# Attention with a step's scores ahead of the preceding pair's transposes and weighted sums, and the right side's tiles at multiples of 256 bytes

## The chip, the cores and the metric

The kernel runs on one core of a Trainium2 chip. The metric is the device time of one execution in microseconds (us). The core has five engines that work at the same time, each through its own list of instructions in order: TensorE (PE) multiplies matrices and also transposes, with PEld as the row of its weight loads; VectorE (DVE) and ScalarE (ACT) do element-wise work and are the only ones that the kernel lets read PE's results; GpSimd (POOL) does element-wise work on SBUF; SyncE (SP) issues most DMAs. SBUF is the on-chip memory of 128 partitions; PSUM holds PE's results in eight banks.

## The reference, cut to what matters

With DEPTH 1 the trunk is a single layer: RMSNorm, 2-D neighbourhood attention and a residual, then RMSNorm, SwiGLU and a residual, then a final RMSNorm. It is applied to a prompt of 1024 tokens and a sample of 512, both of width 1024, on a grid of 64 columns.

```
def neighbourhood_attention(x, w_qkv, rpb, w_o):
    ...
    def row_step(r):
        rs = jnp.clip(r - kh // 2, 0, rows - kh)
        ...
        s = jnp.einsum('bjqhd,bkjchd->bhjqkc', qr, kr).astype(jnp.float32) * scale
        ...
        s = jnp.where(valid_j, s + bias.astype(jnp.float32), -jnp.inf)
        p = jax.nn.softmax(s.reshape(B, NA_HEADS, NA_NCB, NA_QBW, kh * NA_KBW), axis=-1)
        p = p.reshape(s.shape).astype(x.dtype)
        return jnp.einsum('bhjqkc,bkjchd->bjqhd', p, vr)
    o = lax.map(row_step, jnp.arange(rows))
    o = jnp.moveaxis(o, 0, 1).reshape(B, T, D_MODEL)
    return o @ w_o

def swiglu(x, w_gate, w_up, w_down):
    return (jax.nn.silu(x @ w_gate) * (x @ w_up)) @ w_down
```

Sixteen heads of 64 attend within 8 rows; columns are handled in four blocks of 16 queries, each with a band of 32 keys. The values are 32-bit floats.

## The kernel before, in words

**Precision.** Every large product is made of three matmuls on rounded operands: each operand is split into a high part (a cast on ACT) and a low part (the difference, on DVE; `split`, L139 to L145), and `PASS` (L164) names the three pairs of parts.

**Stages.** By the span of the profile: norms, transposes and value projections up to 181 us (`v_tile`, matmuls L281; the values go to HBM as `v_d`); prompt attention from 181 to 519; sample attention from 519 to about 732, with the output projection (`project`, L593) woven in and going on to 797; gate and up products to 1466 (`product`, L824, seven products of a Strassen-like scheme); down products to the end (L1062).

**A step of attention.** `steps` yields, for one head pair `hp` and one group `g` of 8 query rows, two steps. A step holds two units (two column blocks `j`), and each unit two heads. A unit's work is:

- `scores` (L391): for each head three matmuls into a PSUM bank of tag S (L397); then, per head, one reduction on DVE that adds the bias, writes the tile `s` to SBUF and takes the row's extreme (L405), an exponential on ACT with its sum (L408), a reciprocal (L410), and a scaling, on DVE for the first head (L412) and on ACT for the second (L414);
- `flip` (L418): per head three transposes (two for the sample) into an S bank (L423), then the two halves of the eviction to the tile `pT`: the cast on ACT (L426) and the difference on DVE (L427);
- `weighted` (L431): matmuls with the values into two banks of tag V (L434), which both units of the step share.

`collect` (L438) then sums the parts of a step's two V banks: a copy on ACT to `tmp` (L444) and two additions on DVE (L445, L447) to the output tile `oT`, which POOL's queue stores to HBM as `o_d` (L462) when the second step of a group is done.

There are four S banks. A step's scores take all four, and the transposes take all four again. There are two tiles of each kind of output and temporary, and four tiles `s`.

**The order of a step.** `step` (L477) traces: the scores and the softmax of this step's two units; filler; the weighted sums and the collect of the *preceding* step, whose transposes are already in `pT`; then, unit by unit, this step's transposes, each followed by filler. Filler is PE work that does not depend on the step: portions of 6 matmuls of the next head pair's q and k projections (`proj`, L335), and in the sample of the output projection (L593). For a prompt head pair `fill` runs two portions after the scores and one after each unit's transposes.

**What sets the order on the engines.** The program is traced in the order of the Python code. A list scheduler then orders each engine's instructions by their place in the trace and by its own estimate of when inputs and buffers will be ready, so an instruction that it takes to be waiting can be overtaken by later ones of the same engine. On the chip each engine runs its list in order; semaphores guard each use of a buffer.

**Between the steps** `chores` load and split weights and values: `v_split` waits for the DMA of a value tile `vr` from `v_d` (L381; cast at L141 on ACT, difference at L142 on DVE), and `wsplit` splits a weight block into `whl`.

**SBUF.** Pools stand on two sides: most grow up from the bottom, those with `side="right"` down from the top. The first tile of the right side is `edge`, 24 floats for each partition (L89), which nothing reads. Below it lie, in their time, `hTp` (the prompt's normed and transposed tokens), `wo` and `oh`, then `hx`, a part of the weight tiles of the gate and up products (`a2p`, `r2p`, `t4p`), and in the last stage `go`, `gr` and the first three of `wd` and `dr` (`rt`). On the left are among others `hTs`, `whl`, all tiles of attention, `h`, and the rest of `wa`, `ws`, `wd`.

Of the kernel before, what the change touches and what calls it, by code (L numbers as in the profile page):

```python
# [11 lines left out]
F32 = mybir.dt.float32  # L12
# [6 lines left out]
P = 128  # L19
# [36 lines left out]
def body(tc, xp, xs, g_mix, g_ffn, g_fin, w_qkv, rpb, w_o, w_g, w_u, w_d, yp, ys):  # L56
# [8 lines left out]
    es = ExitStack()  # L65
    with es:
# [21 lines left out]
        ident = cpool.tile([P, P + 16], F32, name="ident")[:, :P]  # L88
        edge = es.enter_context(tc.tile_pool(name="edge", bufs=1, side="right")).tile([P, 24], F32, name="edge")  # L89
        nc.gpsimd.memset(edge, 0.0)  # L90
# [300 lines left out]
        def scores(q, k, krow, nrow, j, bias):  # L391
            n = nrow * 32
# [9 lines left out]
            for h, pt in enumerate(pss):  # L402
                s = ap.tile([P, 384], F32, tag="s", name="s", bufs=4)
                mx = stat.tile([P, 1], F32, tag="mx", name="mx")
# [32 lines left out]

        def collect(pos, dst):  # L438
            for h in range(2):
                m, o = (0, HD) if h == 0 else (HD, 0)  # L440
                pv = pos[h].rearrange("p (g z q) -> p g z q", g=2, z=2)
                tmp = ap.tile([P, 2, P], F32, tag="tmp", name="tmp")
                t = tmp[m:m + HD]
                nc.scalar.copy(t, pv[o:o + HD, :, 0])  # L444
                nc.vector.tensor_tensor(t, t, pv[m:m + HD, :, 0], ALU.add)  # L445
                tv = t.rearrange("p g (r i) -> p g r i", i=16)
                nc.vector.tensor_tensor(dst(h), tv, pv[m:m + HD, :, 1].rearrange("p g (r i) -> p g r i", i=16),  # L447
                                        ALU.add)

        def steps(hp, g, q, k, v, n, store):  # L450

            oT = ap.tile([P, 512], F32, tag="o", name="oT", bufs=2)
            ov = oT.rearrange("p (r j i) -> p j r i", r=8, j=NJ)
# [23 lines left out]
        def step(st, fill):  # L477
# [6 lines left out]
            if prev:  # L484
                p, pT = prev.pop()
                pos = [psum("V", "po") for _ in range(2)]
# [3 lines left out]
                if p["done"]:  # L490
                    p["done"]()
            pT = []
            for u, x in enumerate(ss):
                pT.append(flip(x, st["n"]))
                fill(1 + u)
            if st:
                prev.append((st, pT))

# [40 lines left out]
        for hp in range(HP):  # L539
# [13 lines left out]
            def fill(part):  # L553
                run(fillers, 1 if part or last else 2)

# [57 lines left out]
        for hp in range(HP):  # L613
# [7 lines left out]
            def fill(part):  # L621
                run(fillers, 1 if part else 2)
                run(ofill, 1 if part else 2)

# [501 lines left out]
```

## Time and profile before

| | |
|---|---|
| time, median of 3 runs | 1808.15 us (1807.66 to 1812.14) |
| the profiled execution | 1815.71 us |
| its span, first to last instruction | 1813.8 us |
| PE busy | 1749.2 us, 96% |
| DVE busy | 1215.9 us, 67% |
| ACT busy | 870.6 us, 48% |
| POOL busy | 431.2 us, 24% |
| mean granted PE clock | 0.992 |

The span is what the trace shows; the execution's own time has a little around it. The share of busy time is a mean over stages of very different make-up. PE's matmuls are pipelined: one is shown as lasting longer than the distance to the next one's start, so busy time alone does not tell how fast they follow each other. In rows of the timeline the first number is the start, the second the length, `x` the count of merged instructions, and a bracket at the end gives the idle time ahead of the row and what ended it. In rows of waits, the engine and the tile that waited stand left of the arrow, what ended the wait on the right.

### The profile page before, as it was taken

Reading aid. Unit: us, or ns where it says so; the run is one execution under the profiler, and the core shown is the slowest. Engines: PE = TensorE matmul, PEld = TensorE weight load, DVE = VectorE, ACT = ScalarE, POOL = GpSimd, SP = SyncE. Lnnn points to the kernel's source line nnn. Section 1 sums busy time; section 2 is a strip of 40 time slices with the busy share of each in tenths; the row PEclk is TensorE's granted clock in tenths of the full one; section 3 lists DMA queues with packets and bytes.
Section 4 is the critical chain, followed back from the end, with each engine's and each line's share of the span. In section 5 each row is a group of like instructions: output and inputs, shape, how many; then the busy total and the mean of one; then the engine's idle time right before and its main releaser. Section 6 shows DMA issues by size and latency. Waiting matters only on the chain.

```text
span 1813.8 us, 25894 instructions
## 1 busy us (share of the span) xinstructions
PE 1749.2 (96%) x9178; PEld 1527.3 (84%) x9178; DVE 1215.9 (67%) x2267; ACT 870.6 (48%) x1742; POOL 431.2 (24%) x509
## 2 busy tenths in 40 slices
PE   7999999999999999999999999989999999999998
PEld 6888777777777788779999999888999987888886
DVE  4401878788787666667877777988777756446553
ACT  4411777667785555544444445433344335433423
POOL 1111000000130000112424242565424352005300
PEclk9999999999999999999999999999999999999999
DMA  7755333333464453653553634888433269555633
GB/s 237 224 182 168 98 107 109 108 103 106 131 204 149 135 157 111 193 181 119 177 171 111 216 109 146 284 298 275 137 115 122 75 210 324 180 158 165 206 110 107
DMA packets 229858, 295.60 MB, mean 163 GB/s; under 512 B 27648, under 2 KB 173824, under 8 KB 229728
## 3 DMA queue, kind: packets, MB, share of 16 engines
q1 hardware_dynamic: 205744, 215.94, 39.3%
q0 software_dynamic: 21248, 69.62, 10.5%
q10 hardware_dynamic: 2736, 8.39, 1.5%
q8 instruction: 72, 1.18, 0.3%
q14 instruction: 58, 0.48, 0.1%
HBM read 218.45 MB, written 87.97 MB: 169 GB/s over the span
## 4 chain that ended last, share of the span: by engine, by line
PE 69%; DMA 11%; DVE 9%; ACT 4%; issue 4%; SPq 2%; POOL 2%; DVEq 0%; ACTq 0%; POOLq 0%
PE pa L824 16%; PE pd L1062 16%; PE pd L824 8%; PE pg L335 7%; PE pgv L281 7%; DMA vr<-v_d 5%; PE pgo L593 4%; PE pb L824 4%; PE pss L397 3%; SPq L381 2%; PE po L434 1%; PE ptt L423 1%; DMA gr<-gop_d 1%; DMA wt_d<-t 1%; ACT s L408 1%
## 5 line engine op out<-in xcount | busy, mean ns | idle before, releaser
L1062 PE MATMUL pd<-wd,go 128*128 128x512 f32 x1386 | 325.7, 396 | 3.6 <-DVE wd L142 2.6
L1062 PEld LDWEIGHTS pd<-wd,go 128*128 128x128 f32 x1386 | 260.4, 188 | 68.8 <-DVE wd L142 4.9
L824 PE MATMUL pa<-h,ws 128*128 128x384 f32 x1056 | 199.4, 336 | 8.7 <-ACT c L849 7.2
L335 PE MATMUL pg<-hTp,whl 128*128 128x512 f32 x768 | 201.9, 407 | 0.0
L824 PE MATMUL pd<-h,ws 128*128 128x384 f32 x1056 | 197.6, 334 | 0.0
L824 PEld LDWEIGHTS pa<-h,ws 128*128 128x128 f32 x1056 | 183.1, 188 | 12.0 <-ACT c L849 9.2
L824 PEld LDWEIGHTS pd<-h,ws 128*128 128x128 f32 x1056 | 184.3, 188 | 0.0
L142 DVE TENSOR_TENSOR ws<-wt,ws 128x1024 fp32r<-128x1024 f32 x88 | 109.9, 1250 | 90.9 <-ACT ws L141 90.9
L335 PEld LDWEIGHTS pg<-hTp,whl 128*128 128x128 f32 x768 | 139.2, 190 | 34.2 <-issue 7.7
L824 PE MATMUL pa<-h,wa 128*128 128x384 f32 x792 | 151.1, 343 | 8.3 <-DVE c L856 8.3
L824 PEld LDWEIGHTS pa<-h,wa 128*128 128x128 f32 x792 | 141.4, 191 | 10.5 <-DVE c L856 10.5
L593 PE MATMUL pgo<-wo,oh 128*128 128x512 f32 x576 | 139.0, 392 | 1.4 <-DVE oh L142 1.4
L141 ACT CAST go<-gr 128x768 fp32r<-128x768 f32 x84 | 65.7, 782 | 151.6 <-PE pd L1062 106.7
L408 ACT ACTIVATE s<-s,mx 128x384 f32<-128x384 f32 (+1 forms) x192 | 109.1, 570 | 54.8 <-DVE mx L405 54.8
L142 DVE TENSOR_TENSOR wa<-wr,wa 128x512 fp32r<-128x512 f32 x132 | 124.0, 952 | 13.1 <-ACT wa L141 12.1
L142 DVE TENSOR_TENSOR go<-gr,go 128x768 fp32r<-128x768 f32 x84 | 81.6, 972 | 75.0 <-ACT go L141 73.4
L593 PEld LDWEIGHTS pgo<-wo,oh 128*128 128x128 f32 x576 | 107.4, 188 | 24.4 <-DVE oh L142 1.8
L889 POOL DMA_DIRECT2D gop_d<-c x66 | 50.6, 766 | 313.1 <-DVE c L880 313.1
L141 ACT CAST wa<-wr 128x512 fp32r<-128x512 f32 x132 | 81.8, 621 | 88.5 <-PE pb L824 43.5
L141 ACT CAST ws<-wt 128x1024 fp32r<-128x1024 f32 x88 | 92.4, 1051 | 63.3 <-issue 49.7
L335 PE MATMUL pg<-hTs,whl 128*128 128x512 f32 x384 | 105.7, 411 | 2.0 <-DVE q L346 2.0
L824 PE MATMUL pb<-h,wa 128*128 128x384 f32 x528 | 101.0, 339 | 4.3 <-ACT wa L141 4.1
(158 smaller groups left out, 2945.3 us busy)
## 6 DMA issues: line engine op xcount, KB each, us to landing
wr<-ffn_w_gate SPq DMA_DIRECT2D x44, 512.0 KB
wr<-ffn_w_up SPq DMA_DIRECT2D x44, 512.0 KB
wr<-na_w_qkv SPq DMA_DIRECT2D x38, 512.0 KB
gop_d<-gs POOLq DMA_DIRECT2D x88, 192.0 KB, 5.7
gr<-gop_d SPq DMA_DIRECT2D x42, 384.0 KB
gr<-gop_d SPq DMA_DIRECT2D x42, 320.0 KB
gop_d<-c POOLq DMA_DIRECT2D x66, 192.0 KB, 2.5
vr<-v_d SPq DMA_DIRECT2D x192, 64.0 KB
```

The source lines that it names most:

```text
L141: nc.scalar.copy(hi, raw)
L142: nc.vector.tensor_tensor(lo, raw, f32(hi), ALU.subtract)
L281: nc.tensor.matmul(pg, hh[a][:, k, c:c + P], wv[k // 2][b][:, k % 2], start=(k == 0 and i == 0), stop=(k == KB - 1 and i == 2))
L335: nc.tensor.matmul(pg, w[:, a, k, :], h[b][:, k, c:c + 512], start=(k == 0 and i == 0), stop=(k == KB - 1 and i == 2))
L381: nc.sync.dma_start(out=raw[:, j * P:(j + 1) * P], in_=src[:, BS[j]:BS[j] + 32, :])
L397: nc.tensor.matmul(pt[:, :n], q[h * HD:(h + 1) * HD, a, j].rearrange("p r i -> p (r i)"), kv[:, krow:krow + nrow, BS[j]:BS[j] + 32], start ...
L408: nc.scalar.activation(s[:, :n], s[:, :n], AF.Exp, bias=mx, scale=-1.0, accum_out=sm)
L423: nc.tensor.transpose(pt[:, c * P:(c + 1) * P], s[:, c * P:(c + 1) * P], ident)
L593: nc.tensor.matmul(pg, ohs[k // 4][:, a, k % 4], wo[:, b, k, n * 512:(n + 1) * 512], start=(k == 0 and i == 0), stop=(k == KB - 1 and i == 2))
L824: nc.tensor.matmul(bank[:, :HT], a(y, k), b[:, z, k], start=start and k == 0 and i == 0, stop=k == KB // 2 - 1 and i == 2, skip_group_chec ...
L889: nc.gpsimd.dma_start(out=gop_d[i, 3 * c:3 * c + 3, :, p].rearrange("j q t -> q j t"), in_=a.rearrange("q (j t) -> q j t", j=3))
L1062: nc.tensor.matmul(pd, go[:, y, i - a], wds[m, i][:, z], start=(i == 0 and k == 0), stop=(i == NP - 1 and k == 2))
```

## The change

Four things are changed together.

1. In `step`, the transposes, the weighted sums and the collect are all those of the preceding step. The order is now: this step's scores and softmax; filler; the preceding step's first unit's transposes; filler; its second unit's transposes; filler; its weighted sums and collect; filler. What is handed to the next step is the softmax tiles `s`, not `pT`.
2. The tiles `s` are six, the output tile `oT` is one, and the temporary `tmp` is one, allocated once for both heads of a collect.
3. Filler is run at four places instead of three: one portion at each for a prompt head pair and for the sample (two kinds there), and for the last prompt head pair one portion at the first and the third.
4. `edge` has 56 floats in place of 24, so that the tiles of the right side lie 128 bytes lower, at multiples of 256 bytes.

```
-        edge = es.enter_context(tc.tile_pool(name="edge", bufs=1, side="right")).tile([P, 24], F32, name="edge")
+        edge = es.enter_context(tc.tile_pool(name="edge", bufs=1, side="right")).tile([P, 56], F32, name="edge")
...
-                s = ap.tile([P, 384], F32, tag="s", name="s", bufs=4)
+                s = ap.tile([P, 384], F32, tag="s", name="s", bufs=6)
...
         def collect(pos, dst):
+            tmp = ap.tile([P, 2, P], F32, tag="tmp", name="tmp", bufs=1)
             for h in range(2):
                 m, o = (0, HD) if h == 0 else (HD, 0)
                 pv = pos[h].rearrange("p (g z q) -> p g z q", g=2, z=2)
-                tmp = ap.tile([P, 2, P], F32, tag="tmp", name="tmp")
...
-            oT = ap.tile([P, 512], F32, tag="o", name="oT", bufs=2)
+            oT = ap.tile([P, 512], F32, tag="o", name="oT", bufs=1)
...
             ss = [next(x) for x in sc]
             fill(0)
             if prev:
-                p, pT = prev.pop()
+                p, pss = prev.pop()
+                pT = []
+                for u, x in enumerate(pss):
+                    pT.append(flip(x, p["n"]))
+                    fill(1 + u)
                 pos = [psum("V", "po") for _ in range(2)]
                 for u in range(2):
                     weighted(pT[u], [x() for x in p["v"]], p["jj"] * 2 + u, p["n"], pos, u)
                 collect(pos, p["dst"])
                 if p["done"]:
                     p["done"]()
-            pT = []
-            for u, x in enumerate(ss):
-                pT.append(flip(x, st["n"]))
-                fill(1 + u)
+            else:
+                fill(1)
+                fill(2)
+            fill(3)
             if st:
-                prev.append((st, pT))
+                prev.append((st, ss))
...
             def fill(part):
-                run(fillers, 1 if part or last else 2)
+                run(fillers, 0 if last and part % 2 else 1)
...
             def fill(part):
-                run(fillers, 1 if part else 2)
-                run(ofill, 1 if part else 2)
+                run(fillers, 1)
+                run(ofill, 1)
```

## The prediction

> **What bounds the kernel now.** I read the page's head first, then stretches of the span by stage, then TensorE's (PE's) timeline inside a step of attention.
>
> ```profile
> span 1813.8 us, 25894 instructions
> ## 1 busy us (share of the span) xinstructions
> PE 1749.2 (96%) x9178; PEld 1527.3 (84%) x9178; DVE 1215.9 (67%) x2267; ACT 870.6 (48%) x1742; POOL 431.2 (24%) x509
> ```
>
> Busy time in two stretches (PE, PEld, DVE, ACT, POOL, then PE clock, DMA share, GB/s), prompt attention first:
>
> ```profile
> 181.00:519.20 338.20, 325.54 (x1873) 258.80 (x1873) 272.06 (x778) 241.96 (x593) 29.68 (x63) 0.99 0.39 113
> ```
>
> and the gate and up products:
>
> ```profile
> 797.00:1466.00 669.00, 647.72 (x3683) 640.94 (x3682) 523.28 (x675) 288.27 (x470) 261.24 (x260) 0.99 0.52 168
> ```
>
> PE is the bound in both, 96% and 97% busy. Time can come only from PE's waits or from the spacing of its matmuls. Its busy share hides both, since an instruction's modelled duration overlaps the next one's; I therefore go by starts. PE's timeline in prompt attention, first a stalled place:
>
> ```profile
> 240.33 1.62 PE L335 MATMUL pg<-hTp,whl 128*128 128x512 f32 x6
> 242.81 2.19 PE L397 MATMUL pss<-kp,q 64*128 64x384 f32 x12 [0.86 <-DVE pT L427]
> ```
>
> The scores wait for L427, the second half of the eviction of the preceding transposes, which hold the score banks. Now a clean step:
>
> ```profile
> 253.42 1.63 PE L335 MATMUL pg<-hTp,whl 128*128 128x512 f32 x6
> 254.97 1.34 PE L397 MATMUL pss<-kp,q 64*128 64x384 f32 x12
> 256.24 3.06 PE L335 MATMUL pg<-hTp,whl 128*128 128x512 f32 x12
> 259.14 1.59 PE L434 MATMUL po<-pT,v 128*128 128x256 f32 x12
> 260.56 0.82 PE L423 MATMUL ptt<-ident,s 128*128 128x128 f32 x6
> 261.14 1.63 PE L335 MATMUL pg<-hTp,whl 128*128 128x512 f32 x6
> ```
>
> It ends, after six more transposes, at
>
> ```profile
> 263.18 2.57 PE L335 MATMUL pg<-hTp,whl 128*128 128x512 f32 x10
> ```
>
> From 253.42 to 263.18 that is 12 scores, 24 projections, 12 weighted sums and 12 transposes in 9.76 us: PE's floor, 39.0 us for the four steps of a head pair. (The x10 shows that the planner had moved four projections of the next step ahead of its scores.) A whole prompt head pair, from first scores to first scores, takes more:
>
> ```profile
> 222.24:265.68 43.44, 42.33 (x242) 34.02 (x242) 34.17 (x99) 30.14 (x75) 3.25 (x8) 0.96 0.37 107
> ```
>
> 43.4 us, with VectorE (DVE) busy for 34.2 and ScalarE (ACT) for 30.1. Then the last prompt pair, the first sample pair with what precedes it, three sample steps, and seven more:
>
> ```profile
> 481.65:519.24 37.59, 35.50 (x205) 27.79 (x204) 34.37 (x96) 31.61 (x76) 7.44 (x8) 1.00 0.43 133
> 519.24:560.62 41.38, 37.50 (x203) 27.74 (x203) 36.22 (x101) 32.62 (x82) 16.62 (x8) 1.00 0.62 196
> 560.62:607.55 46.93, 43.46 (x225) 34.94 (x224) 29.41 (x84) 23.32 (x61) 2.17 (x4) 0.96 0.45 139
> 607.55:706.88 99.33, 98.46 (x533) 80.68 (x533) 62.73 (x189) 52.24 (x139) 5.42 (x10) 1.00 0.49 147
> ```
>
> In the first two of these DVE itself is nearly full: 34.4 of 37.6 and 36.2 of 41.4. Who waited for whom between 181 and 519 (us in total, times, longest):
>
> ```profile
> ACT v L141 <- DMA vr<-v_d: 15.5, 9, 3.1
> ...
> PE pss L397 <- DVE pT L427: 5.7, 8, 0.9
> PE ptt L423 <- ACT s L414: 5.4, 13, 1.4
> ```
>
> The last two are the edges of the old order: scores wait for the eviction of the transposes before them, and transposes wait for their own step's softmax.
>
> **The change, part by part.**
>
> *The new order of a step.* No matmul is added or removed. Transposes now work on the preceding pair's softmax, a step old, so the wait on L414 goes. Between the last transposes and the next scores lie 6 projections, 12 weighted sums and 6 projections, 1.55 + 1.42 + 1.4 = 4.4 us by the clean step, in place of 1.55. Against this stands the eviction (groups of 181 to 519: busy, mean ns of one):
>
> ```profile
> L408 ACT ACTIVATE s<-s,mx 128x384 f32<-128x384 f32 x128 | 77.3, 605 | 48.0 <-DVE mx L405 48.0
> L405 DVE CUSTOM_DVE_ANT_0 s<-pss,bp 128x384 f32<-128x384 f32 x128 | 65.4, 547 | 1.2 <-PE pss L397 1.1
> L427 DVE TENSOR_TENSOR pT<-ptt,pT 128x384 fp32r<-128x384 f32 x127 | 63.8, 551 | 2.8 <-ACT pT L426 1.2
> ...
> L426 ACT CAST pT<-ptt 128x384 fp32r<-128x384 f32 x128 | 54.1, 486 | 9.4 <-PE ptt L423 8.2
> ```
>
> Two casts and the last subtraction make 0.49 + 0.49 + 0.55 = 1.5 us when neither engine is held up, so the scores' wait goes as well. What is late next is the weighted sum: its second unit has 6 projections and the first unit's 6 sums as cover, 1.4 + 0.7 = 2.1 us, for the same 1.5, and the four exponentials of the new scores can stand ahead of the casts on ACT. I expect part of the old wait to come back there.
>
> What can be had: the seven other prompt pairs take 338.2 - 37.6 = 300.6 us, and their floor is 7 x 39.0 = 273.3, so 27.3. In the last and the first sample pair DVE is the floor: 37.6 - 34.4 + 41.4 - 36.2 = 8.4. The seven sample steps take 14.2 us each and hardly wait, so the three before them hold 46.9 - 42.6 = 4.3. In all 40.0 us. Bounds: 0, if each wait returns elsewhere, to 40. I take 25, some 60%: each old edge gets at least 2.8 us more cover, but DVE would be busy in order for 34.2 of 39.0 us, and ACT's waits for the value loads (the 15.5 us above) are not touched.
>
> *Score tiles 4 to 6.* Two pairs in flight would need eight. So the third and fourth reductions (L405) of a step wait until the first unit's transposes have read two old tiles. That is a new wait, on DVE; reciprocals, scalings and L427 stand behind it, and ACT's exponentials and PE's next transposes wait for those. It ends after 6 projections and 6 transposes, 1.4 + 0.6 = 2.0 us behind the scores, and the first two reductions fill 1.1 of that: some 0.9 us of idle DVE a step, where (39.0 - 34.2) / 4 leaves 1.2. Bounds 0 to 0.9 us a step; I charge nothing apart, but it is part of the 40% that I leave out.
>
> *One output tile and one temporary.* The next collect's L447 now waits until the output's DMA has landed (us, min/median/max of 24):
>
> ```profile
> DMA to landing us min/median/max: 2.2/2.3/4.8
> ```
>
> The tile is needed a step later, 9.76 us when clean. Cost 0, covered by that step; without the cover 2.3 us for each of 24. The single temporary is free a step ahead likewise, and the two heads use different halves of it: 0. Together they free the 3 KB that the two score tiles take, so the left tiles behind stay where they were.
>
> *Filler split* (2+1+1 to 1+1+1+1; in the last pair two portions instead of three): the same matmuls, counted above.
>
> *The edge tile, 24 to 56 floats.* It moves every right-side tile by 128 bytes. As compiled before, the right-side tiles (hTp, wo, oh, go, hx, the a2p copy of wa, wd 0 to 2) start 128 bytes above a multiple of 256; on the left whl, hTs, h, ws, the rest of wa and wd start on a multiple, and wv 128 above one. Uninterrupted runs of 512-column matmuls, start and length first:
>
> ```profile
> 91.71 44.06 PE L281 MATMUL pgv<-wv,hTp 128*128 128x512 f32 x192
> 135.61 22.47 PE L281 MATMUL pgv<-wv,hTs 128*128 128x512 f32 x96
> 157.92 22.94 PE L335 MATMUL pg<-hTp,whl 128*128 128x512 f32 x98
> ```
>
> In the sample's projections, the output projection and the down products:
>
> ```profile
> 523.44 3.79 PE L335 MATMUL pg<-hTs,whl 128*128 128x512 f32 x16
> ```
>
> ```profile
> 775.53 22.03 PE L593 MATMUL pgo<-wo,oh 128*128 128x512 f32 x96
> ```
>
> ```profile
> 1507.60 299.14 PE L1062 MATMUL pd<-wd,go 128*128 128x512 f32 x1285 [0.19 <-DVE go L142]
> ```
>
> Spacing is (length - 0.4) / (count - 1). Where both operands have the same offset: 228.6 ns (wv, hTp), 226.7 (hTs, whl), 227.8 (wo, oh). Where they differ: 232.3 (wv, hTs), 232.4 (hTp, whl), 232.7 (wd, go). After the change hTp agrees with whl: 768 x (232.4 - 226.7) = 4.4 us. go agrees with wd: 1386 x (232.7 - 227.2, the mean of the last two equal pairs) = 7.6. hTp parts from wv: 384 x (232.3 - 228.6) = 1.4 lost. For 384 columns, the second with wa from the right side:
>
> ```profile
> 1473.08 2.24 PE L824 MATMUL pd<-h,ws 128*128 128x384 f32 x12
> 1475.16 2.27 PE L824 MATMUL pa<-h,wa 128*128 128x384 f32 x12
> ```
>
> 2.27 - 2.24 over 11 is 2.7 ns each, for 528 such and 264 with hx 2.1 us. Together 12.7; I take 12, all on PE's path. Bounds 0 to 12.7.
>
> [...]
>
> *Clock.* Twice in attention PE ran at half speed for 3.4 us, once
>
> ```profile
> 245.37:248.78 3.41, 3.41 (x10) 2.64 (x9) 3.34 (x13) 2.89 (x9) 0.30 (x1) 0.50 0.41 114
> ```
>
> and once near 594. Each costs 1.7 us, comes behind a wait, and is part of the excess above; nothing more is booked.
>
> **Sum.** 25 + 12 = 37 us off the profiled span of 1813.8 make 1776.8. The profiled execution took 1815.71, 7.6 above the median of the runs, so for the runs 1808.15 - 37 = 1771.
>
> **Rivals.**
>
> 1. *All of the excess goes.* For it: DVE and ACT have room in a pair of 39 us. Against: DVE in order at 88%. 1808 - 40 - 12 = 1756.
> 2. *Only the spacing gains.* The planner had already moved projections into the waits (the x10), and the weighted sums now wait in place of the scores. 1808 - 12 = 1796.
> 3. *The offsets do nothing*; spacing depends on something that the tiles keep, such as which tile streams. Only the order gains: 1808 - 25 = 1783. Against: go with wd differs from wo with oh, though all four roles are alike. [...]
> 4. *Slower: weighted sums behind ACT's order.* Place: L434's second unit, which needs L427 and, before it, L426. If ACT works off four exponentials and two scalings (6 x 0.6) and four casts (4 x 0.49) first, that and the last subtraction are 6.1 us, as long as PE's way from scores to there (4.2 of projections, 1.2 of transposes, 0.7 of sums). Then all of ACT's other work in a step (30.1 / 4 - 5.6 = 1.9) and its waits for value loads (15.5 / 32 = 0.5) delay PE: 9.8 + 2.4 = 12.2 us a step against 10.8, 39 lost in 28 steps, 12 gained: 1835. It decides from 1.7 us a step. Against: the planner fills such waits with the fourth portion of projections, 1.4 us.
>
> **How the numbers follow.** Forecast 0.56 (its own range 1760 to 1782), rival 1 0.15, rival 2 0.14, rival 3 0.08, rival 4 0.07. The range 1748 to 1797 takes in rivals 1 to 3, with some 8 us below the first for bounds that are themselves read from single stretches, and leaves rival 4 out. Under 0.3% (5.4 us) a measurement of this kernel can't tell from no change. Faster 0.89: all but rival 4 and 0.04 of rival 2, where losses eat the spacing's gain too; same 0.04; slower 0.07.
>
> **What would show it.** Right: the waits of L397 on L427 and of L423 on L414 nearly gone; prompt pairs at 40 to 41 us; L1062's long run at 227 ns a matmul (292 us for 1285), hTp with whl at 227, and L281 with hTp up at 232. New waits, if any, stand before L434 on L427 and on DVE before L405 on PE's L423. Wrong: L1062 still at 232.7; prompt pairs at 43 us or more; L434 waiting 1.7 us a step; L447 waiting for the landing of o_d.

## The result, and the profile after

The changed kernel takes 1822.98 us (median of 5 runs, 1817.84 to 1826.03) against 1810.28 of the kernel before on the same chip (5 runs, 1807.66 to 1812.14). The ratio is 1.0062 with a 95% interval of 1.0039 to 1.0084: slower by about 0.6%, where 1771 us was forecast. The profiled execution took 1817.84 us, with a span of 1816.0; that is the fastest of the changed kernel's five, while the execution profiled before, 1815.71, lay above all of its five runs. So the two traces differ by 2 us only, and the medians by 12.7.

Each stage of the changed kernel's span: length, then busy time of PE, PEld, DVE, ACT and POOL, then PE clock, DMA share and GB/s. The rows are seven prompt pairs, the last prompt pair, the sample up to the first scores of its last pair, the rest of the output projection, gate and up, down (from `step` on, line numbers are higher by up to 4 than before, so L517 becomes L521):

```profile
180.97:476.87 295.90, 286.21 (x1660) 222.34 (x1660) 240.47 (x679) 206.86 (x513) 19.94 (x55) 1.00 0.39 112
476.87:521.55 44.68, 40.87 (x216) 29.91 (x215) 36.66 (x100) 33.70 (x80) 7.63 (x8) 0.92 0.44 136
521.55:716.12 194.57, 182.74 (x950) 144.18 (x949) 128.20 (x368) 106.46 (x278) 22.17 (x22) 0.97 0.48 145
716.12:808.64 92.52, 90.45 (x457) 74.93 (x457) 59.97 (x131) 44.93 (x90) 13.16 (x22) 1.00 0.45 151
808.64:1488.04 679.40, 658.08 (x3745) 650.57 (x3743) 530.87 (x683) 290.93 (x475) 266.21 (x264) 0.99 0.52 170
1488.04:1816.00 327.96, 317.89 (x1386) 261.69 (x1386) 181.63 (x245) 130.16 (x219) 68.50 (x80) 0.98 0.57 188
```

The same stretches in the four profiled executions that separate the two halves of the change (the middle two are the first two experiments below), in us:

| stage | before | offsets alone | order alone | after |
|---|---|---|---|---|
| up to the first scores | 181.1 | 181.1 | 180.6 | 181.0 |
| seven prompt pairs | 300.6 | 298.4 | 294.1 | 295.9 |
| last prompt pair | 37.6 | 37.6 | 44.7 | 44.7 |
| sample, to its last pair's scores | 187.6 | 188.1 | 196.5 | 194.6 |
| rest of the output projection | 90.5 | 90.5 | 94.8 | 92.5 |
| gate and up | 680.7 | 681.4 | 680.4 | 679.4 |
| down | 335.7 | 327.7 | 335.2 | 328.0 |
| span | 1813.8 | 1804.8 | 1826.5 | 1816.0 |

The down products win 7.7 us by the offsets. The order wins 2.5 (at the new offsets) to 6.5 us (at the old) in seven pairs, of which about 1.1 is only moved: 12 of the 336 transposes now run behind the last of them. Another 1.7 is one stretch at half clock (3.41 us at 0.50, from 245.37 us on) that lies in the seven pairs of the trace before and has no like there in the trace after. The order loses 7.1 us in the last pair (the moved transposes among them), 6.5 to 8.9 in the sample, and 2.0 to 4.3 behind it.

What PE waited for between 181 and 521.5 (us in total, times, longest), and the largest wait of its weight loads:

```profile
PE ptt L423 <- DVE mx L405: 9.1, 20, 0.8
PE po L434 <- DVE pT L427: 3.4, 8, 1.8
...
PEld ptt L423 <- DVE mx L405: 23.3, 42, 1.2
```

The two waits of the old order are gone, as forecast, and the one expected before the weighted sums is there. The first and the last row were not foreseen: the transposes of the preceding step take the four S banks that the new scores have just filled, so they wait until the reductions L405 have read them. One such place in the timeline (PE and DVE):

```profile
272.12 1.33 PE L397 MATMUL pss<-kp,q 64*128 64x384 f32 x12
272.25 0.41 DVE L447 TENSOR_TENSOR oT<-tmp,po 64x256 f32<-64x256 f32 x1
272.71 0.42 DVE L445 TENSOR_TENSOR tmp<-tmp,po 64x256 f32<-64x256 f32 x1
273.32 0.69 DVE L346 TENSOR_TENSOR q<-pg,q 128x512 fp32r<-128x512 f32 x1 [0.19 <-ACT q L345]
273.38 1.66 PE L335 MATMUL pg<-hTp,whl 128*128 128x512 f32 x6
274.05 0.43 DVE L447 TENSOR_TENSOR oT<-tmp,po 64x256 f32<-64x256 f32 x1
274.50 0.69 DVE L142 TENSOR_TENSOR v<-vr,v 128x512 fp32r<-128x512 f32 x1
275.22 0.56 DVE L405 CUSTOM_DVE_ANT_0 s<-pss,bp 128x384 f32<-128x384 f32 x1
```

The scores are done at 273.4, but the first reduction begins at 275.22: the collect, an eviction of projections and a value tile's difference stand before it. The transposes have one portion of projections as cover, 1.66 us, and it doesn't reach.

### The profile page after: what moved, and what is told of

The parts are those of the page before. It is cut to its first block, busy times and chain, and to the rows that moved or that the text cites. A ratio compares the mean times of both kernels' runs of the same rounds, so it can differ in the third digit from the quotient of the medians.

```text
span 1816.0 us, 25869 instructions
## 1 busy us (share of the span) xinstructions
PE 1746.8 (96%) x9178; PEld 1521.6 (84%) x9178; DVE 1226.7 (68%) x2267; ACT 868.4 (48%) x1742; POOL 429.1 (24%) x509
## 4 chain that ended last, share of the span: by engine, by line
PE 54%; DVE 7%; DMA 4%; issue 3%; ACT 2%; POOL 2%; SPq 1%; POOLq 0%; DVEq 0%; ACTq 0%
PE pd L1066 17%; PE pa L828 15%; PE pd L828 7%; PE pgo L597 4%; PE pb L828 4%; PE pg L335 3%; DMA vr<-v_d 2%; PE po L434 1%; PE pss L397 1%; DVE wa L142 1%; PE ptt L423 1%; DMA t<-ffn_w_down 1%; POOL gop_d L893 1%; DVE c L884 0%; DVE ws L142 0%
## 5 line engine op out<-in xcount | busy, mean ns | idle before, releaser
L1066 PE MATMUL pd<-wd,go 128*128 128x512 f32 x1386 | 317.9, 392 | 3.7 <-DVE wd L142 2.9
L335 PE MATMUL pg<-hTp,whl 128*128 128x512 f32 x768 | 206.5, 404 | 0.0
L142 DVE TENSOR_TENSOR ws<-wt,ws 128x1024 fp32r<-128x1024 f32 x88 | 112.2, 1276 | 90.7 <-ACT ws L141 90.7
L597 PE MATMUL pgo<-wo,oh 128*128 128x512 f32 x576 | 142.8, 395 | 1.3 <-DVE oh L142 1.3
L142 DVE TENSOR_TENSOR wa<-wr,wa 128x512 fp32r<-128x512 f32 x132 | 124.0, 952 | 12.4 <-ACT wa L141 11.4
L142 DVE TENSOR_TENSOR go<-gr,go 128x768 fp32r<-128x768 f32 x84 | 81.9, 975 | 70.6 <-ACT go L141 69.2
L141 ACT CAST ws<-wt 128x1024 fp32r<-128x1024 f32 x88 | 92.5, 1052 | 64.1 <-issue 50.0
L141 ACT CAST wa<-wr 128x512 fp32r<-128x512 f32 x132 | 81.8, 621 | 85.4 <-PE pb L828 43.3
L335 PE MATMUL pg<-hTs,whl 128*128 128x512 f32 x384 | 111.1, 419 | 4.7 <-DVE q L346 2.3
```

The source lines that it names most:

```text
L141: nc.scalar.copy(hi, raw)
L142: nc.vector.tensor_tensor(lo, raw, f32(hi), ALU.subtract)
L335: nc.tensor.matmul(pg, w[:, a, k, :], h[b][:, k, c:c + 512], start=(k == 0 and i == 0), stop=(k == KB - 1 and i == 2))
L597: nc.tensor.matmul(pg, ohs[k // 4][:, a, k % 4], wo[:, b, k, n * 512:(n + 1) * 512], start=(k == 0 and i == 0), stop=(k == KB - 1 and i == 2))
L1066: nc.tensor.matmul(pd, go[:, y, i - a], wds[m, i][:, z], start=(i == 0 and k == 0), stop=(i == NP - 1 and k == 2))
```

## The experiments

Times are medians; each ratio is to the kernel before, run on the same chip in the same session (there 1810 to 1815 us).

**The offsets alone**, old order:

```
-... tile([P, 24], F32, name="edge")
+... tile([P, 56], F32, name="edge")
```

> The kernel before with the edge tile of 56 floats alone; order and tiles as before. Theory (the spacing gains, the new order loses): the same matmuls at 227 instead of 232 ns on L1062, L335 and L824, about 12 us less, so near 1798 against 1810 of the kernel before, and all of the change's loss lies in the order. Rival (a PE that runs closer together meets more stretches at half clock, which eat the gain): 1806 to 1810, the starts at 227 ns all the same.

1804.54 us, ratio 0.9945 (0.9926 to 0.9964): 10 us faster. The down products, in one uninterrupted run each, for the offsets alone and then for the order alone:

```profile
1479.99 317.71 PE L1062 MATMUL pd<-wd,go 128*128 128x512 f32 x1385 [2.40 <-DVE wd L142]
```

```profile
1494.08 325.30 PE L1066 MATMUL pd<-wd,go 128*128 128x512 f32 x1385 [2.37 <-DVE wd L142]
```

7.6 us between them, the term as forecast. Of hTp's 4.4 us only 2.2 arrive in the prompt, where PE waits anyway, and nothing of L824's 2.1: twelve matmuls with wa now take 2.24 us as well, but the stage is no shorter (681.4 us against 680.7). Why stays open.

**The order alone**: the changed kernel with the edge tile of 24 floats.

```
-... tile([P, 56], F32, name="edge")
+... tile([P, 24], F32, name="edge")
```

> The changed kernel with the edge tile of 24 floats: the new order, six score tiles, single output and temporary tiles, filler split, old offsets. Theory (the order loses what the offsets gain): 1823 + 12 = 1835, prompt pairs near 43 us, the last prompt pair near 44. Rival (the offsets gain nothing in the end, the order loses 12): 1823.

1824.67 us, ratio 1.0063 (1.0045 to 1.0082). The order loses 11 us. In the spans the two halves add up (1826.5 against 1816.0), in the times they don't: 1.0063 and 1.0062. The changed kernel's five runs had granted clocks of 0.985 to 0.990, this one's six 0.987 to 0.993. Among those five the time rises by 8.2 us from the run at 0.989 to the one at 0.985. By that slope the medians' clocks, 0.987 and 0.9915, make some 9 us, as an estimate, most of the gain that is missing. That the faster PE gave its gain back in half-speed stretches fits this; why it met more of them is not shown.

**The collect a step later**:

```
             ss = [next(x) for x in sc]
+            flush()
             fill(0)
...
-                collect(pos, p["dst"])
-                if p["done"]:
-                    p["done"]()
+                late.append((pos, p))
```

> The changed kernel with the collection of a step's weighted sums (L444 to L447 and the output's store) traced one step later, behind the next step's scores and reductions; nothing left out. Theory (the transposes L423 wait for the reductions L405, which free the four score banks and stand on DVE behind the collection): the 33 us of waits of L423 on L405 between 181 and 521 shrink to under 10, a prompt pair takes about 40.5 instead of 42.5 us, the time falls by some 16 to 1807. Rival (the time is lost for want of filler ahead of the weighted sums): prompt pairs stay above 42, 1823.

1814.59 us, ratio 1.0005 (0.9992 to 1.0017). Faster than the change by some 10 of the 16 us expected, but not for the reason given: the waits of L423 on L405 stayed (8.3 us of PE, 23.2 of its weight loads), and pairs from the second on took 42.5 to 43.3 us. (`flush` collects what `late` holds.) The scheduler put part of the collect ahead of the reductions again, and L346 and L142 stood there as before; the single output tile now made L447 wait 10.4 us for the landing of `o_d`. Its clocks, 0.988 to 0.993, lie above the change's, so a part of the 10 us may be fewer half-speed stretches. It does not decide on the theory.

**Filler at all four places of the last pair**:

```
-                run(fillers, 0 if last and part % 2 else 1)
+                run(fillers, 1)
```

> The changed kernel with one portion of projections at each of the four places of a step in the last prompt pair too, instead of at the second and fourth place's none; nothing left out. Theory (the banks' edge): the weighted sums get cover, but the transposes wait as before; last prompt pair 43 to 44.7 us, 1821 to 1823. Rival (the split of the filler is at fault): last prompt pair 37 to 40 instead of 44.7, 1816 to 1818.

1822.29 us, ratio 1.0045 (1.0031 to 1.0059); the last pair took 46.4 us instead of 44.7. The split is not what it lost.

**Cover moved to the transposes**:

```
-                run(fillers, 0 if last and part % 2 else 1)
+                run(fillers, 0 if last and part % 2 else (2, 1, 1, 0)[part])
```

> The changed kernel with the portions of projections in a prompt step split 2, 1, 1, 0 instead of 1, 1, 1, 1 (the last prompt pair as changed): two portions between the scores and the first transposes, none behind the weighted sums; nothing left out. Theory (cover at the wrong place: the portion and the 12 sums behind the evictions hide nothing, while the transposes have one portion of cover against four reductions): waits of L423 on L405 from 32 us to under 12 between 181 and 521, prompt pairs from 42.3 to about 41, 1813 against 1822. Rival (ACT's and DVE's work in order is the bound of a step): the wait moves to the weighted sums, pairs stay at 42 or more, 1820 to 1825.

1820.68 us, ratio 1.0039 (1.0024 to 1.0055). What PE waits for between 181 and 478:

```profile
PE po L434 <- DVE pT L427: 14.0, 18, 2.2
PE pss L397 <- ACT kp L352: 0.2, 1, 0.2
```

The transposes no longer wait, and the weighted sums wait for 14.0 us instead: the wait moves, as the rival had it. That points to work behind PE that is late, whatever PE's order.

**New order in seven prompt pairs only**, the old one from the last prompt pair on:

```
-        def step(st, fill):
+        def step(st, fill, old=False):
...
+            if old:
+                pT = []
+                for u, x in enumerate(ss):
+                    pT.append(flip(x, st["n"]))
+                    fill(1 + u)
+                if st:
+                    prev.append((st, pT, True))
+            else:
+                fill(3)
+                prev.append((st, ss, False))
```

> The changed kernel with the old order (scores, weighted sums of the preceding pair, own transposes) and the old split of the filler in the last prompt pair and the sample; new order in the seven other prompt pairs; six score tiles, single output and temporary tiles and new offsets stay; nothing left out. Theory (the new order loses only where there is little filler): last prompt pair 37 to 39 instead of 44.7 us, sample and what follows as in the kernel with the offsets alone, 1802 against 1804.5 of that one. Rival (the loss there comes from the single output tile or the order of the queues, which stay): last pair and sample stay long, 1812 to 1822.

1808.44 us, ratio 0.9971 (0.9959 to 0.9982). The sample takes 188.9 us and the rest of the output projection 90.6, as with the offsets alone. So the loss there is the order's; the six score tiles and the single output and temporary tiles, which stay, cost nothing in the old order. The last pair still takes 42.3 us, since the switch falls into it. Over the old order with the same offsets (0.9945) nothing is won.

**wv's offset too**, old order:

```
-            fill = vp.tile([P, 480], F32, ...)
+            fill = vp.tile([P, 512], F32, ...)[:, :480]
```

> The kernel before with the edge tile of 56 floats, and wv's tiles moved by 128 bytes to a multiple of 256 as well (a constant tile ahead of them takes 512 floats instead of 480); order as before. Theory (spacing goes by the offset of both operands): L281 at 227 instead of 232 ns for 576 matmuls, 2.9 us less than the offsets alone, 1801.5. Rival (which of the two tiles moved is what counts): 1804.5.

1807.72 us, ratio 0.9960 (0.9947 to 0.9974), no better in time than the offsets alone. In the trace the term is there: the first scores begin at 178.5 us instead of 181.1, and V's projection of the sample, which took 22.47 us for 96 before, runs at (21.92 - 0.4) / 95 = 226.5 ns:

```profile
134.15 21.92 PE L281 MATMUL pgv<-wv,hTs 128*128 128x512 f32 x96
```

**A third offset**, 192 bytes above a multiple of 256 on the right side, in one execution:

```
-... tile([P, 24], F32, name="edge")
+... tile([P, 40], F32, name="edge")
```

> The kernel before with the edge tile of 40 floats: the right side starts 192 bytes above a multiple of 256 instead of 128 above one. Theory (a pair of operands is slow where their offsets by 256 bytes differ): the down products and hTp with whl stay at 232 ns, V's projection of the prompt goes to 232, 1811 to 1813. Rival (it goes by 64 bytes, or by the difference's size): the spacing of these takes another value than 227 or 232 ns.

1816.78 us. The down products stay slow, and hTp with whl takes a value of its own:

```profile
157.52 22.60 PE L335 MATMUL pg<-hTp,whl 128*128 128x512 f32 x98
...
1508.55 299.26 PE L1062 MATMUL pd<-wd,go 128*128 128x512 f32 x1285 [0.27 <-DVE go L142]
```

(299.26 - 0.4) / 1284 is 232.8 ns, but (22.60 - 0.4) / 97 is 228.9, between the two. In long runs of 512 columns equal offsets took 227.0 ns for hTp with whl and 226.7 for go with wd (both after the change; the second is (305.48 - 0.4) / 1346) and 226.5 for wv with hTs, unequal ones 232.4, 232.7 and 232.3 before. What an unequal pair costs is not a single number.

**Scaling of the scores on POOL**, in the changed kernel:

```
-                if h == 0:
-                    nc.vector.tensor_scalar(s[:, :n], s[:, :n], ri, None, ALU.mult)
-                else:
-                    nc.scalar.mul(s[:, :n], s[:, :n], ri)
+                nc.gpsimd.tensor_scalar(s[:, :n], s[:, :n], ri, None, ALU.mult)
```

> The changed kernel with the scaling of the scores by their reciprocal sums (L412 on DVE, L414 on ACT) done by POOL for both heads; nothing left out. It takes 0.84 us of DVE's and 1.1 us of ACT's time out of each prompt step. Theory (cover at the wrong place): waits of L423 on L405 change by less than a fifth, pairs above 41.5, 1819 to 1823. Rival (ACT's and DVE's work in order is the bound of a step): pairs near 40, 1806 to 1812. If POOL's queue makes the scaling late, the transposes wait for it and the time is over 1825.

1811.27 us, ratio 0.9982 (0.9966 to 0.9997): it falls between both expectations. Less work on DVE and ACT helps, in the last pair above all (40.8 us instead of 44.7); the pairs from the second to the seventh of its trace took 42.4 to 43.9 us, in an execution with a mean clock of 0.986.

**Differences of value and unscaled weight tiles on POOL**, in the changed kernel, in the old order with the offsets, and with the new order in seven pairs only:

```
-                nc.vector.tensor_tensor(lo, raw, f32(hi), ALU.subtract)
+                (eng or nc.vector).tensor_tensor(lo, raw, f32(hi), ALU.subtract)
...
+            split(r, ..., scale, nc.gpsimd)
...
+            split(rv, ..., None, nc.gpsimd)
```

> The changed kernel with the differences of the value tiles and of the unscaled weight tiles (L142 of v and whl, some 30 us of DVE's time in the eight prompt pairs) done by POOL; nothing left out. Theory (the reductions L405 come late because splits and evictions stand before them in DVE's queue): waits of L423 on L405 between 181 and 478 from 8.1 (PE) and 20.5 us (its weight loads) to under half, prompt pairs from 42.3 to about 41, 1810 to 1814 against 1822. Rival (the order of DVE's other work takes up the room, or POOL's slower differences make the weighted sums wait): pairs at 42 or more, 1819 to 1825.

> The kernel before with the new offsets and wv's moved too, and the same differences on POOL; old order. Theory (the old order's waits come from DVE's late evictions too): some 3 to 6 us less than without, 1800 to 1804 where the new offsets alone have 1804 to 1808. Rival (the old order isn't held by DVE's load): no difference, 1806.

> New order in seven prompt pairs alone, old order from the last prompt pair on, new offsets, and the differences of value and unscaled weight tiles on POOL. Theory (the reductions come late behind DVE's splits): prompt pairs about 41 instead of 42.2 us, 1799 to 1803 against 1808 without POOL. Rival: pairs stay, 1807 to 1809.

1814.83 us (ratio 1.0014, 1.0000 to 1.0028), 1799.98 (0.9939, 0.9922 to 0.9956) and 1803.92 (0.9957, 0.9944 to 0.9971). The changed kernel's reductions come in time now, but the weighted sums wait (181 to 478):

```profile
PE po L434 <- DVE pT L427: 8.7, 18, 1.3
PE ptt L423 <- DVE mx L405: 1.6, 2, 1.4
```

From the second pair on, three of a pair's four steps took 9.6, 9.8 and 10.7 us (from first scores to first scores), the second 11.2 to 11.8. That step in the timeline, in the changed kernel with POOL's help:

```profile
323.35 0.62 ACT L141 CAST v<-vr 128x512 fp32r<-128x512 f32 x1 [1.30 <-DMA vr<-v_d]
323.88 0.47 ACT L426 CAST pT<-ptt 128x384 fp32r<-128x384 f32 x1
...
324.38 0.56 DVE L427 TENSOR_TENSOR pT<-ptt,pT 128x384 fp32r<-128x384 f32 x1 [1.87 <-ACT pT L426]
...
324.99 0.62 PE L434 MATMUL po<-pT,v 128*128 128x256 f32 x3 [1.26 <-DVE pT L427]
```

ACT stands still for a value tile's load, and the casts L426 of the eviction stand behind it. The kernel before, at the stall that the prediction began with:

```profile
238.83 0.62 ACT L141 CAST v<-vr 128x512 fp32r<-128x512 f32 x1 [1.70 <-DMA vr<-v_d]
239.49 0.69 DVE L142 TENSOR_TENSOR v<-vr,v 128x512 fp32r<-128x512 f32 x1 [2.16 <-ACT v L141]
...
240.00 0.76 ACT L444 COPY tmp<-po 64x256 f32<-64x256 f32 x2
...
240.78 1.63 ACT L426 CAST pT<-ptt 128x384 fp32r<-128x384 f32 x4
241.30 0.87 DVE L447 TENSOR_TENSOR oT<-tmp,po 64x256 f32<-64x256 f32 x2
242.20 1.95 DVE L427 TENSOR_TENSOR pT<-ptt,pT 128x384 fp32r<-128x384 f32 x4
```

It is a value tile's load again. Behind it on ACT come the cast, a scaling L414, the collect's copies L444 and only then the casts L426; on DVE the collect's additions, which need those copies, stand before L427. The scores' wait on L427 at 242.81 was the end of a chain that began with a DMA in ACT's queue. This made the next theory.

**Casts of the value tiles on POOL too**, so that ACT's queue meets no value load; in the old order, in the new one, and with the new one in seven pairs only:

```
-                nc.scalar.copy(hi, raw)
+                nc.gpsimd.tensor_copy(hi, raw) if cast else nc.scalar.copy(hi, raw)
```

> The kernel before with the new offsets (wv's too), the differences of value and unscaled weight tiles on POOL, and the casts of the value tiles (L141 of v) on POOL as well, so that ACT's queue never waits for a value load. Theory (in the second step of each pair the casts L426 stand behind a value load in ACT's queue): that step goes from 11.3 to about 9.9 us, some 10 us in all, 1790 against 1800 with the casts on ACT. Rival (the scores' wait is that of the old order, too little cover for the evictions): the step stays above 11, 1798 to 1802. If POOL makes the values late, the weighted sums wait for them instead.

> The changed kernel with the same work on POOL, casts of the value tiles too. Theory (the value load in ACT's queue): the second step of each pair from 11.6 to about 10.1 us and L434's waits on L427 from 8.7 us to under 3, 1804 against 1815 with the casts on ACT. Rival (the new order gives the evictions too little cover): the step stays above 11, 1812 to 1816.

> New order in seven prompt pairs alone, old order from the last pair on, offsets with wv's, value tiles wholly and unscaled weight differences on POOL. Theory (with the value load out of the way both orders come near PE's floor): as the old order throughout with the same, within 4 us of it. Rival (the new order is worth something of its own, some 1 us a pair): 5 to 9 us less than that.

1818.35 us (ratio 1.0038, 1.0025 to 1.0051), 1802.05 (0.9951, 0.9933 to 0.9968) and 1789.79 (0.9884, 0.9866 to 0.9901). From the second pair on, the second step of a pair fell to 9.8 us in all three, from 11.0 to 13.4 in the old order, 11.2 to 11.8 in the new one and 11.3 to 13.7 with the new one in seven pairs. In the new order the waits of L434 on L427 went from 8.7 to 2.4 us, in the old one those of L397 on L427 from 7.3 to 1.0. The theory holds for that step in both orders. The casts' own time on ACT is not the reason: in the new order the first and third steps hold value casts too, with no wait for a load above 0.3 us, and took 9.6 to 9.8 us with and without them. But the old order lost 2.6 to 6 us in each third step:

```profile
292.23 0.56 DVE L405 CUSTOM_DVE_ANT_0 s<-pss,bp 128x384 f32<-128x384 f32 x1 [3.96 <-DMA bp<-es_d]
...
293.72 0.55 PE L423 MATMUL ptt<-ident,s 128*128 128x128 f32 x3 [2.06 <-DVE s L412]
```

A reduction waits for a bias; behind it the softmax and the step's own transposes.

**The bias memset on DVE**, in the old order and in the kernel with the new order in seven pairs:

```
-                nc.gpsimd.memset(b[0:HD, :, 256:384], FILL)
+                nc.vector.memset(b[0:HD, :, 256:384], FILL)
```

> The old order throughout with the new offsets (wv's too) and the value tiles on POOL, as before, but the memset in the prompt's biases (L207, L211) on DVE instead of POOL. Theory (the third step's loss is POOL's queue): that step falls from 12.4 to 15.8 us back to about 9.8, seven prompt pairs take 7 x 39.3 = 275 to 280 us, 1780 to 1786, as good as the new order in the prompt or better. Rival (the old order itself is late with the softmax ahead of its own transposes): L423 goes on waiting for L412, the step stays above 11.5, 1800 or more.

> New order in seven prompt pairs, old from the last pair on, value tiles on POOL, the biases' memset on DVE. Theory: no wait for a bias was left there, so as without: 1788 to 1791. Rival (POOL's queue made biases late here too): the first pair's third step, 13.7 us, falls to about 10 and the time to 1784.

1816.77 us (ratio 1.0018, 1.0002 to 1.0033) and 1786.75 (0.9852, 0.9828 to 0.9876). The old order's third step stayed at 12.3 to 14.5 us: POOL's queue was not the cause. One such place in the old order (SP's queue and DVE):

```profile
287.88 1.12 SPq L381 DMA_DIRECT2D vr<-v_d  x2
289.05 0.60 SPq L212 DMA_DIRECT2D bp<-in_d  x1
289.69 0.60 SPq L213 DMA_DIRECT2D bp<-es_d  x1
...
290.67 0.56 DVE L405 CUSTOM_DVE_ANT_0 s<-pss,bp 128x384 f32<-128x384 f32 x1 [4.19 <-DMA bp<-es_d]
```

The bias's loads stand in SP's queue behind a value tile's.

**Those loads ahead of the value loads**, old order throughout:

```
                     step(st, fill)
+                    fill_bias()
                     for _ in range(2):
```

> The old order throughout, value tiles on POOL and the prompt biases' memset on DVE as in the kernel before it, with the loads of the next biases issued ahead of the step's value loads. Theory (the third step's loss is the bias loads behind a value load in SP's queue, not the old order): that step falls from 12.3 to 14.5 us to about 9.8, seven prompt pairs to 275 to 282 us, 1780 to 1790, so that the new order is worth nothing of its own in the prompt (280.0 us there). Rival (the old order, whose transposes wait for their own step's softmax, has no room for a late bias): the step stays above 11, 1800 or more, and the new order's gain is that it bears later reductions.

1791.54 us, ratio 0.9872 (0.9849 to 0.9895). A whole prompt pair of this kernel, and then of the one before it with the new order:

```profile
262.44:301.86 39.42, 39.42 (x242) 32.62 (x242) 32.57 (x100) 28.40 (x71) 11.12 (x11) 1.00 0.40 117
```

```profile
259.01:298.99 39.98, 39.88 (x242) 32.34 (x241) 32.72 (x100) 27.70 (x71) 10.95 (x11) 1.00 0.39 116
```

The old order comes to 39.4 us a pair and the new one to 40.0. Over seven pairs that is 280.6 us and 280.0, since the first pair of the old order took 44.1. With the queues clear the new order is worth nothing of its own in the prompt. The two kernels' times, 0.9872 and 0.9852, are not told apart by their intervals. Both beat the kernel before and the change, by 1.3 to 1.5% and by some 2%.

## Why the prediction was wrong

**What bounds the kernel.** PE bound, going by starts, the two named waits: right. The floor was nearly so: a pair without a wait took 39.42 us against 39.0, though with matmuls closer together than where the floor was read. DVE, busy there for 32.6 of 39.4 us, held nothing up. Its full load in the kernel before did: with the differences on POOL, a pair's third step in the old order went from 10.6 to 9.8 us.

**The order, -25 us: the step that failed.** The seven pairs' excess of 27.3 us was read as the price of two edges in PE's order, and 60% of it was taken as the new order's gain; the other two terms were 8.4 and 4.3 us. Measured: 11 us lost. In the seven pairs the order gained 1.4 to 5.4 us beside the moved transposes, against 16; in the last pair it lost 7.1, and in and behind the sample 8.5 to 13. Two things stand in place of that step.

First, the wait of the scores on L427 was followed back one instruction only. Behind L427 stood L426 and the collect, behind these a value tile's cast, and behind that a load. The prediction quoted ACT's 15.5 us of waits for value loads and said that the order did not touch them; it did not see that the scores' wait began with them. In the new order the same load holds up the weighted sums. Taking the value tiles off ACT's queue took 1.2 us or more from the second step of each pair in either order.

Second, the four S banks. The prediction let the next transposes wait for the reductions only by way of the six score tiles, at most 0.9 us of idle DVE a step, and charged nothing apart for it. But the transposes of the preceding step follow the new scores directly in those banks, so the old edge from eviction to scores became an edge from reduction to transposes, with one portion of 1.66 us as cover. The 12 weighted sums and the last portion now stand where PE waits for nothing. With two portions ahead of the transposes, the wait moved on to the weighted sums (14.0 us).

**Last pair and sample.** The forecast took 60% of 8.4 us as gained. (What it calls the first sample pair holds 48 scores, so two pairs.) There is little filler there, and the two edges come to PE bare. The new order's last pair, with what held the eviction up:

```profile
478.63 4.83 POOL L521 TENSOR_TENSOR wo<-oraw,wo 128x1024 fp32r<-128x1024 f32 x2 [7.66 <-ACT wo L520]
481.09 2.58 DVE L412 TENSOR_SCALAR s<-s,ri 128x384 f32<-128x384 f32 x1
...
486.08 0.59 PE L434 MATMUL po<-pT,v 128*128 128x256 f32 x3 [1.76 <-DVE pT L427]
```

The long scaling is not the new order's own. The kernel before has one in its last pair, and there PE's transposes waited 0.84 us behind it:

```profile
486.31 2.26 DVE L412 TENSOR_SCALAR s<-s,ri 128x384 f32<-128x384 f32 x1
```

Of the last pair's 7.1 us, PE's idle time makes 1.7 (3.8 us against 2.1), a half-speed stretch of 6.83 us 3.4, and the moved transposes 1.1. In the sample PE is idle for 11.8 us against 8.2, and three half-speed stretches of 3.41 us stand against one, at 1.7 us each. Aside from the span's end, the trace after has eleven of them (two pairs joined), that before seven. Why PE idles longer in the sample was not taken apart further. One candidate is the six score tiles: the reductions there waited 9.5 us, in 11 waits, for transposes that had yet to read them. No kernel with eight was run.

**Score tiles, output and temporary tiles, filler split, all at 0:** right in the prompt, where no reduction waited for a transpose and no L447 for a landing, and where two other splits changed little (1.0045 and 1.0039 against 1.0062). In the sample the score tiles' share is open, as said.

**The offsets, -12 us:** right in kind; 10 measured (0.9926 to 0.9964). The down products' 7.6 came whole. The terms of the prompt and of L824 were mis-sized: 2.2, since the prompt is not held by spacing while PE waits there, and nothing. The 226.7 ns for hTs with whl come out as 226.0 by the prediction's own rule, from 16 matmuls; hTp with whl ran at (22.42 - 0.4) / 97 = 227.0 ns after the change.

**Clock, nothing booked:** wrong by the four stretches more in the trace, 1.7 us each. The clocks of the other executions speak for more of them still (the estimate under the order alone).

**Rivals.** The fourth, slower by weighted sums behind ACT's order, had the sign, at a chance of 0.07. Its mechanism made 3.4 us of waits only where it asked for 1.7 us a step. No case held the banks.

## What to carry to other kernels

Follow a wait back until it ends at something that is late by itself, a load or a queue, before giving its length to the order of the engine that shows it; here an in-order ACT queue passed a DMA's lateness on to whichever matmul came next (in the row at 323.35 ACT was idle for 1.30 us for a load, and at 324.99 PE for 1.26 ahead of L434). When work is reordered on shared buffers, list for each buffer who must let go of it in the new order, and ask what now covers that. The wait that moved here from the transposes to the weighted sums when cover was shifted (14.0 us there) had its cause behind PE.

## What the runs showed of the hardware

**Stretches at half speed.** In the trace after, PE's clock fell to 0.50 for stretches of 3.41 us or two of them joined, at nine places aside from the span's end. PE's longest single wait ahead was 1.8 to 3.2 us at eight of these; the stretch from 815.61 us on followed a wait of 3.92. Stretches of the changed kernel around three such places (length and PE's busy time first, the clock third from the right), and from 588.33 on one that half speed did not follow at once:

```profile
484.52:487.93 3.41, 1.85 (x9) 1.24 (x9) 1.95 (x4) 1.97 (x5) 0.00 (x0) 1.00 0.07 22
487.93:494.76 6.83, 6.83 (x23) 5.13 (x23) 3.41 (x9) 2.34 (x5) 0.86 (x2) 0.50 0.12 43
588.33:591.74 3.41, 1.41 (x10) 1.13 (x9) 2.49 (x4) 2.07 (x6) 0.00 (x0) 1.00 0.04 13
591.74:595.15 3.41, 2.68 (x12) 1.88 (x10) 1.68 (x4) 0.37 (x2) 0.00 (x0) 1.00 0.64 188
593.75:597.16 3.41, 1.18 (x7) 0.51 (x6) 1.21 (x2) 1.43 (x3) 0.00 (x0) 1.00 0.54 159
597.16:600.57 3.41, 3.18 (x13) 2.57 (x14) 3.12 (x10) 1.81 (x5) 0.54 (x1) 0.50 0.77 231
699.56:702.97 3.41, 1.47 (x7) 1.24 (x7) 2.67 (x7) 1.48 (x5) 0.54 (x1) 1.00 0.27 70
...
702.97:706.39 3.42, 3.42 (x12) 2.73 (x11) 0.83 (x4) 1.26 (x5) 0.00 (x0) 0.50 0.74 239
```

PE was busy for 1.2 to 1.9 of the 3.41 us ahead of each of the three half-speed stretches, and the longest single waits there were 1.8, 2.0 and 2.3 us. At a clock of 0.50 each stretch of 3.41 us costs 1.7 us. From 588.33 us on PE was busy for 1.41 us, with a longest wait of 2.00, and the clock of the next 3.41 us was 1.00: what sets a stretch off is not shown. A stretch lowers the mean clock by some 0.001 (1.7 of 1816 us), so the changed kernel's clocks of 0.985 to 0.990 stand for some five stretches more or fewer, as an estimate.

**DVE beside POOL.** A scaling of 0.42 us took 2.58 us while POOL worked off a difference of two SBUF tiles (the rows at 478.63 and 481.09 above). The scaling began at 481.09, while the second of POOL's two differences ran (481.06 to 483.46), and ended at 483.67, 0.21 us after it. In the kernel before the like scaling of 2.26 us (486.31 to 488.57) ended 0.21 us after POOL's second difference (485.86 to 488.36). What holds the scaling up is not shown. Even so, moving some 30 us of DVE's differences to POOL (19.3 of value and 9.8 of weight tiles between 181 and 478 in the changed kernel) paid in the new order (1.0014 against 1.0062); in the old one the intervals overlap (0.9939 against 0.9960).
